# A sliding-window copy on one core: early tiles made of two columns, another mix of skipped rows, a second queue for the last stores

## The chip, the core and the metric

The kernel runs on one core of one Trainium2 chip. The metric is device time in microseconds, the median of several executions. The core has a vector engine (DVE), a scalar engine (ACT), GpSimd (POOL), a sync engine (SP) and a tensor engine that is not used here. Sixteen DMA engines move data between the memory outside (DRAM) and the 128 partitions of the memory on the chip. DMAs are issued by SP, ACT or POOL, each on its own queue; an indirect DMA, whose rows go to addresses read from an index tile, is issued by POOL.

## The reference

All windows of 8 x 8, at stride 4, are copied out of an input of 16 batches, 64 channels and 64 x 64 points. Nothing is calculated; each input value appears in up to four windows.

```python
batch, c, h, w = x.shape                       # 16, 64, 64, 64, float32
n_h = (h - window_size) // stride + 1          # 15
n_w = (w - window_size) // stride + 1          # 15
for i in range(n_h):
    for j in range(n_w):
        result[:, i, j] = x[:, :, 4*i:4*i + 8, 4*j:4*j + 8]
```

The input has 16.8 MB and the output 59.0 MB. One window of one batch, 64 channels x 64 values, is a row of 16 KB that lies in one piece in the output: 3600 such rows.

## The kernel before, in words

**Where the input lies.** The whole input is loaded once into the tile L (L49). A partition holds one channel half (ch, 32 channels), one batch and one quarter of the image height (q, 16 rows of points): partition = 64 ch + 32 y + 4 b + q, where y is the batch half and b one of its eight batches. The 16 rows of a quarter begin four windows, called slots s = 0 to 3; slot 3 needs rows of the next quarter also, and the last quarter has no slot 3.

**Loads.** L104 to L110 load y by y and q by q. Of channel half 0, SP issues channels SMALL to 31 and POOL the first SMALL channels (L54, SMALL = 4); POOL issues all of channel half 1. Each such load writes 8 partitions in pieces of 4 KB.

**Output tiles.** G is four tiles of 128 partitions x 4096 values, 16 KB in each partition: 128 output rows. tile_ (L160) hands them out in turn, so a tile's next use waits until its last store has landed. fill (L135) copies the two channel halves of one output row out of L, on ACT (act) and DVE (dve); copies of slot 3 take a copy and a stream_shuffle on DVE (L146, L147), which fetches from the next partition. scatter (L123) is one indirect DMA from POOL that sends the partitions of a tile to the rows named in an index tile; an index past the end makes it skip that row.

**Which tiles there are.** unit(j, 0) is a "plain" tile: column j, slots 0 and 1 of everything, 128 rows. unit(j, 2) is a "crossed" tile: slots 2 and 3; the last quarter has no slot 3, so 16 of its rows are skipped. In crossed tiles either partitions 64 to 127 hold slot 3 (idx_hi) or partitions 0 to 63 do (idx_lo); L182 chooses: 9 times idx_hi, 6 times idx_lo. part(y, j) is a tile of one batch half only, which can begin before the other half is loaded: 64 rows are filled and 64 skipped, by an index moved past the end (L89 to L93). The four tiles are filled with zeros first (L154 to L157), so that skipped partitions hold something.

**Order.** L188 to L199: part(0, j) for j = 0, 1, 2; then part(1, j) and a plain tile, three times; then two crossed tiles and a plain one, over and over: 32 scatters. Column 14 of slots 0 and 1 comes last: two tiles, each stored by four plain DMAs of 16 rows from SP (L214). tile_ is called once without use ahead of them. All stores write rows of their own and are declared free of each other.

The DMAs of POOL share eight completion semaphores in turn. A load or scatter waits until the one eight earlier has landed.

Of the kernel before, what the change touches and what calls it, by code (L numbers as in the profile page):

```python
# [10 lines left out]
def kernel(  # L11
# [7 lines left out]
    nc = tc.nc  # L19
    P = nc.NUM_PARTITIONS  # L20

    B, C, H, W = x.shape
    Bo, NH, NW, Co, WSo, WSo2 = out.shape
    WS = int(window_size)
    ST = int(stride)
    assert Bo == B and Co == C and WSo == WS and WSo2 == WS

    f32 = mybir.dt.float32
    i32 = mybir.dt.int32
    ALU = mybir.AluOpType  # L30
    CH = 2
    HQ = P // (B * CH)
    CL = C // CH
    RB = H // HQ
    NSLOT = RB // ST
    NWIN = NH * NW
    CFREE = C * WS * WS
    HP = P // CH
    YB = 8
    NY = B // YB  # L40
    QP = YB * HQ
# [3 lines left out]
    ipool = ctx.enter_context(tc.tile_pool(name="ipool", bufs=1))  # L45
# [3 lines left out]
    L = lpool.tile([P, CL, RB, W], f32)  # L49
# [1 line left out]

    SMALL, HWP = 4, 8  # L54

    def load(eng, ch, y, q, c0, c1):
        p0 = ch * HP + y * QP + q
# [4 lines left out]
    def itile(name):  # L62
        return ipool.tile([P, 1], i32, name=name)

    pi, tb, tq, tc_, th, idx, idx_y0, idx_y1, idx_lo, idx_hi = (
        itile(n) for n in ("pi", "tb", "tq", "tc", "th", "idx", "idx_y0", "idx_y1", "idx_lo", "idx_hi")
    )
    FAR = float(2 * B * NWIN)
    nc.gpsimd.iota(pi[:, :], pattern=[[0, 1]], base=0, channel_multiplier=1)  # L69

    def bits(d, shift, mask):
        nc.vector.tensor_scalar(out=d[:, :], in0=pi[:, :], scalar1=shift, scalar2=mask, op0=ALU.logical_shift_right, op1=ALU.bitwise_and)  # L72

    def mul(d, a, m):
        nc.vector.tensor_scalar(out=d[:, :], in0=a[:, :], scalar1=float(m), scalar2=None, op0=ALU.mult)  # L75

    def tt(d, a, b, op):
        nc.vector.tensor_tensor(out=d[:, :], in0=a[:, :], in1=b[:, :], op=op)  # L78
# [8 lines left out]
    tt(idx, tb, th, ALU.add)  # L87

    bits(th, 5, 1)  # L89
    mul(th, th, FAR)  # L90
    tt(idx_y0, idx, th, ALU.add)
    nc.vector.tensor_scalar(out=th[:, :], in0=th[:, :], scalar1=-1.0, scalar2=FAR, op0=ALU.mult, op1=ALU.add)
    tt(idx_y1, idx, th, ALU.add)  # L93

    nc.vector.tensor_scalar(out=tq[:, :], in0=tq[:, :], scalar1=float(HQ - 1), scalar2=FAR, op0=ALU.is_equal, op1=ALU.mult)
    tt(th, tc_, tq, ALU.mult)
# [17 lines left out]
    NG = 4  # L114
    G = [gpool.tile([P, C, WS, WS], f32, name=f"G{n}") for n in range(NG)]

    o_q = out.rearrange("b i j c r w -> i j b (c r w)")

    def free(st):
        tc.declare_no_dep(st.ins, group="stores", reason="each store writes rows of its own")  # L120
        tc.add_to_no_dep_group("stores", st.ins)

    def scatter(g, ix, j, s):  # L123
        st = nc.gpsimd.indirect_dma_start(  # L124
            out=o_v,
            out_offset=bass.IndirectOffsetOnAxis(ap=ix[:, 0:1], axis=0),
            in_=g.rearrange("p c r w -> p (c r w)"),
            in_offset=None,
            element_offset=(s * NW + j) * CFREE,
            bounds_check=B * NWIN - 1,  # L130
            oob_is_err=False,
        )
        free(st)

    def fill(g, half, s, j, lo, n, copies):  # L135

        d = slice(half * HP + lo, half * HP + lo + n)
        cols = slice(j * ST, j * ST + WS)
        for ch in (half, 1 - half):
            f = slice(ch * HP + lo, ch * HP + lo + n)  # L140
            cs = slice(ch * CL, (ch + 1) * CL)
            copy = copies[ch != half]
            if s < NSLOT - 1:
                copy(out=g[d, cs, :, :], in_=L[f, :, s * ST : s * ST + WS, cols])  # L144
            else:
                copy(out=g[d, cs, 0:ST, :], in_=L[f, :, s * ST : RB, cols])  # L146
                nc.vector.stream_shuffle(out=g[d, cs, ST:WS, :], in_=L[f, :, 0:ST, cols], mask=nxt)  # L147

    act, dve = nc.scalar.copy, nc.vector.tensor_copy

    EARLY = NG - 1
    zero = ipool.tile([P, 1], f32, name="zero")  # L154
    nc.vector.memset(zero[:, :], 0.0)  # L155
    for g in G:
        act(out=g.rearrange("p c r w -> p (c r w)"), in_=zero.to_broadcast([P, CFREE]))  # L157
    at = 0

    def tile_():  # L160
        nonlocal at
        at += 1
        return G[(at - 1) % NG]

    def part(y, j):
        g = tile_()
        for half in range(CH):
            fill(g, half, half, j, y * QP, QP, (dve, dve) if y and half else (act, dve))
        scatter(g, (idx_y0, idx_y1)[y], j, 0)

    crossed = 0

    def unit(j, s):
        nonlocal crossed
        g = tile_()
        if s == 0:
            for half in range(CH):
                fill(g, half, half, j, 0, HP, (act, dve))
            scatter(g, idx, j, s)
        else:  # L180

            turn = int(crossed % 5 in (1, 3))  # L182
            crossed += 1
            fill(g, turn, s, j, 0, HP, (act, act))
            fill(g, 1 - turn, s + 1, j, 0, HP, (dve, dve))
            scatter(g, (idx_hi, idx_lo)[turn], j, s)

    for j in range(EARLY):  # L188
        part(0, j)
    plain = [(j, 0) for j in range(EARLY, NW - 1)]  # L190
    cross = [(j, 2) for j in range(NW)]
    for j in range(EARLY):
        part(1, j)
        unit(*plain.pop(0))
    while plain:
        for w in cross[:2]:
            unit(*w)
        cross = cross[2:]
        unit(*plain.pop(0))  # L199


    j = NW - 1
    tile_()
    for s in range(2):
        g = tile_()
        cols = slice(j * ST, j * ST + WS)
        for y in range(NY):
            d = slice(QP + y * QP, QP + (y + 1) * QP)
            for ch, copy in enumerate((act, dve)):
                f = slice(ch * HP + y * QP, ch * HP + (y + 1) * QP)  # L210
                copy(out=g[d, ch * CL : (ch + 1) * CL, :, :], in_=L[f, :, s * ST : s * ST + WS, cols])  # L211
        g_q = g.rearrange("p c r w -> p (c r w)")
        for q in range(HQ):
            free(nc.sync.dma_start(out=o_q[q * NSLOT + s, j], in_=g_q[QP + q : QP + q + (B - 1) * HQ + 1 : HQ]))  # L214


# [33 lines left out]
```

## Time and profile before

| What | Value |
|---|---|
| median of 3 runs | 194.87 us (194.72 to 194.99) |
| the profiled execution | 194.68 us, of it 192.9 us span |
| DVE busy | 110.2 us (57%), 153 instructions |
| ACT busy | 138.3 us (72%), 70 instructions |
| POOL busy | 54.6 us (28%), 53 instructions |
| ACT copies of L144 | 61, 1896 ns each |
| DVE copies of L144 | 37, 1224 ns each |
| zero fills on ACT, L157 | 4, 3600 ns each |
| ACT_TABLE_LOAD, L157 | 1, 1283 ns, at 0.74 us |

The span is the time from the first to the last instruction of the profiled execution. An engine's busy time says how much it worked, not that it set the time: what matters is which of them the others waited for in each stretch. "idle before, releaser" tells what ended an engine's waits:

```profile
L144 ACT COPY G<-L 64x2048 f32<-64x2048 f32 (+1 forms) x61 | 115.3, 1896 | 40.0 <-issue 20.7
L147 DVE STREAM_SHUFFLE G<-L 64x1024 f32<-64x1024 f32 x30 | 38.3, 1277 | 0.0
L124 POOL DMA_INDIRECT out_dram<-G,idx_hi x9 | 12.0, 1338 | 34.9 <-DVE G L147 24.5
L157 ACT COPY G<-zero 128x4096 f32<-128x4096 f32 x4 | 14.1, 3600 | 0.0
```

Each line gives the source line, the engine, what is written and read, how often; then busy time, the mean of one in ns, and the idle time just before.

### The profile page before, as it was taken

Reading aid. Unit: us, or ns where it says so; the run is one execution under the profiler, and the core shown is the slowest. Engines: PE = TensorE matmul, PEld = TensorE weight load, DVE = VectorE, ACT = ScalarE, POOL = GpSimd, SP = SyncE. Lnnn points to the kernel's source line nnn. Section 1 sums busy time; section 2 is a strip of 40 time slices with the busy share of each in tenths; the row PEclk is TensorE's granted clock in tenths of the full one; section 3 lists DMA queues with packets and bytes.
Section 4 is the critical chain, followed back from the end, with each engine's and each line's share of the span. In section 5 each row is a group of like instructions: output and inputs, shape, how many; then the busy total and the mean of one; then the engine's idle time right before and its main releaser. Section 6 shows DMA issues by size and latency. Waiting matters only on the chain.

```text
span 192.9 us, 487 instructions
## 1 busy us (share of the span) xinstructions
DVE 110.2 (57%) x153; ACT 138.3 (72%) x70; POOL 54.6 (28%) x53
## 2 busy tenths in 40 slices
DVE  5000007700999979876876875874974794723330
ACT  8993008940897879999778777877977797754560
POOL 7402212531166430422214123134043124320000
DMA  2999999999989999999999999999999999999764
GB/s 79 337 404 400 399 401 397 401 401 407 421 357 418 404 423 421 425 421 404 426 425 428 420 411 418 432 435 411 404 435 418 425 431 404 418 432 435 321 292 177
DMA packets 11588, 75.81 MB, mean 393 GB/s; under 512 B 3888, under 2 KB 3888, under 8 KB 7984
## 3 DMA queue, kind: packets, MB, share of 16 engines
q0 software_dynamic: 9472, 66.34, 83.8%
q1 hardware_dynamic: 2112, 9.44, 12.4%
q14 instruction: 4, 0.03, 0.0%
HBM read 16.78 MB, written 69.21 MB: 446 GB/s over the span
## 4 chain that ended last, share of the span: by engine, by line
DMA 73%; DVE 12%; issue 7%; POOL 2%; ACTq 1%; ACT 1%; DVEq 0%; PEldq 0%
DMA out_dram<-G,idx 34%; DMA out_dram<-G,idx_hi 22%; DMA L<-in_x_dram 16%; DVE G L144 9%; POOL L L58 2%; DVE G L146 2%; DVE G L147 2%; ACTq L245 1%; ACT G L211 1%; DVEq L144 0%; POOL pi L69 0%; DVEq L146 0%; PEldq L245 0%; ACTq L211 0%
## 5 line engine op out<-in xcount | busy, mean ns | idle before, releaser
L144 ACT COPY G<-L 64x2048 f32<-64x2048 f32 (+1 forms) x61 | 115.3, 1896 | 40.0 <-issue 20.7
L144 DVE COPY G<-L 64x2048 f32<-64x2048 f32 (+1 forms) x37 | 45.0, 1224 | 41.9 <-DMA L<-in_x_dram 27.1
L147 DVE STREAM_SHUFFLE G<-L 64x1024 f32<-64x1024 f32 x30 | 38.3, 1277 | 0.0
L146 DVE COPY G<-L 64x1024 f32<-64x1024 f32 x30 | 21.6, 720 | 21.5 <-DMA out_dram<-G,idx 16.2
L124 POOL DMA_INDIRECT out_dram<-G,idx_hi x9 | 12.0, 1338 | 34.9 <-DVE G L147 24.5
L58 POOL DMA_DIRECT2D L<-in_x_dram x16 | 11.4, 715 | 23.9 <-DMA L<-in_x_dram 23.4
L124 POOL DMA_INDIRECT out_dram<-G,idx x11 | 12.4, 1126 | 18.6 <-ACT G L144 15.9
L124 POOL DMA_INDIRECT out_dram<-G,idx_lo x6 | 8.9, 1480 | 24.1 <-DVE G L147 17.0
L124 POOL DMA_INDIRECT out_dram<-G,idx_y x6 | 9.6, 1603 | 16.0 <-ACT G L144 8.9
L157 ACT COPY G<-zero 128x4096 f32<-128x4096 f32 x4 | 14.1, 3600 | 0.0
L211 ACT COPY G<-L 32x2048 f32<-32x2048 f32 x4 | 7.6, 1896 | 7.4 <-DMA out_dram<-G,idx 4.9
L211 DVE COPY G<-L 32x2048 f32<-32x2048 f32 x4 | 4.9, 1220 | 10.1 <-DMA out_dram<-G,idx 6.6
L157 ACT ACT_TABLE_LOAD x1 | 1.3, 1283 | 0.7 <-PEq L231 0.7
L155 DVE MEMSET zero<- 128x1 f32 x1 | 0.1, 59 | 0.8 <-PEq L231 0.8
L78 DVE CUSTOM_DVE_ANT_0 idx_y<-idx,th 128x2 uint16<-128x2 uint16 x2 | 0.3, 160 | 0.1
L78 DVE TENSOR_TENSOR th<-tc,tq 128x1 int32<-128x1 int32 x2 | 0.3, 158 | 0.1
L75 DVE TENSOR_SCALAR th<-tc 128x1 int32<-128x1 int32 x2 | 0.3, 154 | 0.0
L69 POOL IOTA pi<- 128x1 int32 x1 | 0.1, 125 | 0.4 <-PEq L245 0.4
L72 DVE TENSOR_SCALAR tb<-pi 128x1 int32<-128x1 int32 x1 | 0.2, 154 | 0.1
L147 DVE LOAD_MASK_SELECT G<-L x30 | 0.2, 6 | 0.0
L78 DVE CUSTOM_DVE_ANT_0 idx_hi<-idx,th 128x2 uint16<-128x2 uint16 x1 | 0.2, 160 | 0.0
L78 DVE CUSTOM_DVE_ANT_0 idx<-tb,th 128x2 uint16<-128x2 uint16 x1 | 0.2, 159 | 0.0
(16 smaller groups left out, 2.2 us busy)
## 6 DMA issues: line engine op xcount, KB each, us to landing
L<-in_x_dram POOLq DMA_DIRECT2D x8, 1024.0 KB, 21.0
L<-in_x_dram SPq DMA_DIRECT2D x8, 896.0 KB
out_dram<-G SPq DMA_DIRECT2D x8, 256.0 KB
L<-in_x_dram POOLq DMA_DIRECT2D x8, 128.0 KB, 21.1
out_dram<-G,idx POOLq DMA_INDIRECT x11, 14.5
out_dram<-G,idx_hi POOLq DMA_INDIRECT x9, 14.1
out_dram<-G,idx_y POOLq DMA_INDIRECT x6, 9.8
out_dram<-G,idx_lo POOLq DMA_INDIRECT x6, 12.9
```

Source lines behind the costliest of these rows:

```text
L58: eng.dma_start(out=L[p0 : p0 + QP - HQ + 1 : HQ, c0:c1, :, :], in_=x_v[ch, y, q, :, c0:c1, :])
L69: nc.gpsimd.iota(pi[:, :], pattern=[[0, 1]], base=0, channel_multiplier=1)
L72: nc.vector.tensor_scalar(out=d[:, :], in0=pi[:, :], scalar1=shift, scalar2=mask, op0=ALU.logical_shift_right, op1=ALU.bitwise_and)
L75: nc.vector.tensor_scalar(out=d[:, :], in0=a[:, :], scalar1=float(m), scalar2=None, op0=ALU.mult)
L78: nc.vector.tensor_tensor(out=d[:, :], in0=a[:, :], in1=b[:, :], op=op)
L124: st = nc.gpsimd.indirect_dma_start(out=o_v, out_offset=bass.IndirectOffsetOnAxis(ap=ix[:, 0:1], axis=0), in_=g.rearrange("p c r w -> p (c ...
L144: copy(out=g[d, cs, :, :], in_=L[f, :, s * ST : s * ST + WS, cols])
L146: copy(out=g[d, cs, 0:ST, :], in_=L[f, :, s * ST : RB, cols])
L147: nc.vector.stream_shuffle(out=g[d, cs, ST:WS, :], in_=L[f, :, 0:ST, cols], mask=nxt)
L157: act(out=g.rearrange("p c r w -> p (c r w)"), in_=zero.to_broadcast([P, CFREE]))
L211: copy(out=g[d, ch * CL : (ch + 1) * CL, :, :], in_=L[f, :, s * ST : s * ST + WS, cols])
L245: with _tile.TileContext(nc) as tc:
```

## The change

- SMALL is 1: SP loads 31 channels of channel half 0 and POOL one.
- part(y, j) fills all 128 partitions: for its batch half, slots 0 and 1 of columns j and j + 1, in eight copies of 32 partitions, four on ACT and four on DVE. The index tiles idx_y0 and idx_y1 name rows of both columns (column + 1 in place of batch + 8), and none is skipped. It is called for j = 0, 2, 4, so the six early tiles cover columns 0 to 5, and plain tiles begin at column 6. There are 29 scatters.
- The zero fills are gone.
- Crossed tiles take idx_hi and idx_lo in turn (8 and 7), and three of them stand between two plain ones.
- Of the last four DMAs two are issued by ACT, two by SP.

```diff
-    SMALL, HWP = 4, 8
+    SMALL, HWP = 1, 8
...
     bits(th, 5, 1)
-    mul(th, th, FAR)
-    tt(idx_y0, idx, th, ALU.add)
-    nc.vector.tensor_scalar(out=th[:, :], in0=th[:, :], scalar1=-1.0, scalar2=FAR, op0=ALU.mult, op1=ALU.add)
-    tt(idx_y1, idx, th, ALU.add)
+    mul(idx_y0, th, 1 - YB * NWIN)
+    tt(idx_y0, idx_y0, idx, ALU.add)
+    nc.vector.tensor_scalar(out=idx_y1[:, :], in0=idx_y0[:, :], scalar1=float(YB * NWIN), scalar2=None, op0=ALU.add)
...
-    EARLY = NG - 1
-    zero = ipool.tile([P, 1], f32, name="zero")
-    nc.vector.memset(zero[:, :], 0.0)
-    for g in G:
-        act(out=g.rearrange("p c r w -> p (c r w)"), in_=zero.to_broadcast([P, CFREE]))
+    EARLY = 3
...
     def part(y, j):
         g = tile_()
-        for half in range(CH):
-            fill(g, half, half, j, y * QP, QP, (dve, dve) if y and half else (act, dve))
+        for d in range(P // QP):
+            s, dj = d // NY, d % NY
+            cols = slice((j + dj) * ST, (j + dj) * ST + WS)
+            for ch in range(CH):
+                f = (ch * NY + y) * QP
+                (act, dve)[(d + ch) % 2](
+                    out=g[d * QP : (d + 1) * QP, ch * CL : (ch + 1) * CL, :, :],
+                    in_=L[f : f + QP, :, s * ST : s * ST + WS, cols],
+                )
         scatter(g, (idx_y0, idx_y1)[y], j, 0)
...
-            turn = int(crossed % 5 in (1, 3))
+            turn = crossed % 2
...
-    for j in range(EARLY):
-        part(0, j)
-    plain = [(j, 0) for j in range(EARLY, NW - 1)]
+    for n in range(EARLY):
+        part(0, 2 * n)
+    plain = [(j, 0) for j in range(2 * EARLY, NW - 1)]
     cross = [(j, 2) for j in range(NW)]
-    for j in range(EARLY):
-        part(1, j)
+    for n in range(EARLY):
+        part(1, 2 * n)
         unit(*plain.pop(0))
     while plain:
-        for w in cross[:2]:
+        for w in cross[:3]:
             unit(*w)
-        cross = cross[2:]
+        cross = cross[3:]
         unit(*plain.pop(0))
...
-            free(nc.sync.dma_start(out=o_q[q * NSLOT + s, j], in_=g_q[QP + q : QP + q + (B - 1) * HQ + 1 : HQ]))
+            free((nc.sync, nc.scalar)[s * q % 2].dma_start(out=o_q[q * NSLOT + s, j], in_=g_q[QP + q : QP + q + (B - 1) * HQ + 1 : HQ]))
```

## The prediction, made blind

> **What bounds the kernel now.** I read the page first (its slices, DMA packets and queues), then the stretches of time, then the timeline of POOL and ACT, and last the completion records of the trace, in which each of the 16 DMA engines reports the end of its share of a transfer.
>
> ```profile
> DMA  2999999999989999999999999999999999999764
> DMA packets 11588, 75.81 MB, mean 393 GB/s; under 512 B 3888, under 2 KB 3888, under 8 KB 7984
> q0 software_dynamic: 9472, 66.34, 83.8%
> q1 hardware_dynamic: 2112, 9.44, 12.4%
> ```
>
> The DMA engines are busy from the second slice to the 37th. They are the bound; ACT and DVE only have to feed them. The change moves the same 75.81 MB, so it can win only where the engines idle (the start, one dip, the last three slices) or where one carries more than another.
>
> ```profile
> 25.00:46.00 21.00, 7.11 (x6) 10.99 (x6) 7.43 (x6) 1.00 1.04 397
> 46.00:54.00 8.00, 5.90 (x5) 5.61 (x3) 1.52 (x1) 1.00 1.04 426
> 54.00:60.00 6.00, 5.84 (x6) 5.90 (x5) 3.46 (x3) 1.00 0.85 352
> 60.00:176.00 116.00, 83.69 (x112) 92.82 (x49) 33.91 (x27) 1.00 1.01 422
> 176.00:187.00 11.00, 4.88 (x4) 7.58 (x4) 0.00 (x0) 1.00 0.79 331
> 187.00:193.00 6.00, 0.00 (x0) 0.00 (x0) 0.00 (x0) 1.00 0.48 202
> ```
>
> The last two columns are DMA share and GB/s. Loads run at 397 GB/s, or 24.8 an engine: 0.165 us for a 4 KB packet. Scatters run at 422, or 26.4 an engine: 0.62 us for a 16 KB row. The dip is at 54 to 60 us (0.85: 0.9 us lost). At the end the share falls to 0.79 and 0.48: half of the engines are done. In the completion records, eight engines end the last scatter at 180.4 us, seven at 186.6 to 186.9, one at 188.5; the last transfer ends on seven at 191.0 and on that one at 192.0.
>
> ```profile
> 14.49 0.66 POOL L58 DMA_DIRECT2D L<-in_x_dram  x1 [4.81 <-DMA L<-in_x_dram]
> 21.20 0.66 POOL L58 DMA_DIRECT2D L<-in_x_dram  x1 [4.87 <-DMA L<-in_x_dram]
> 28.05 0.66 POOL L58 DMA_DIRECT2D L<-in_x_dram  x1 [4.86 <-DMA L<-in_x_dram]
> 34.91 1.31 POOL L58 DMA_DIRECT2D L<-in_x_dram  x1 [3.99 <-DMA L<-in_x_dram]
> 29.52 11.01 ACT L144 COPY G<-L 32x2048 f32<-32x2048 f32 x6 [13.36 <-issue]
> 50.27 11.51 ACT L144 COPY G<-L 64x2048 f32<-64x2048 f32 x6 [0.46 <-DMA out_dram<-G,idx_y]
> ```
>
> POOL reissues a load when the one eight earlier has landed, so its lines show the landings of the first batch half: a round every 6.8 us, the last at 34.6. ACT starts its copies at 29.52, when channel half 0 is there. One ACT copy costs 11.01/6 = 1.84 us early and 11.51/6 = 1.92 us later.
>
> [...] POOL's large loads end on one half 5.2 us apart (32 packets at 0.163). [...] q0's 9472 packets less 3472 rows, 2304 load packets, 768 reports and 624 skipped rows leave 2304 empty packets, one in group A for each load packet in B and the reverse. A round on A is 4 small packets and 4 of SP's, then 32 empty ones turn about with 32 of SP's: 40 x 0.165 = 6.6 us, seen 6.8. [...]
>
> **SMALL 4 to 1.** A round on A becomes 1 + 1, then 32 + 32 with 34 data packets: 6 x 0.165 = 1.0 us less. Channel half 1 of the first batch half (34.6) is whole 4 rounds, 4.0 us, earlier: 30.6. For half 0 the small loads end at 29.2 - 4.0 = 25.2. SP's fourth load ended at 25.1 after 112 of its packets and 12 of POOL's; now it is 124 and 4, four slots more: 25.1 + 0.7 + 0.2 for empty packets = 26.0. Each engine still carries 256 load packets, so the second half stays at about 47.8 and scatter data begins at 46.7 as before.
>
> **Zero fills out, table load moved.** The four fills (14.1 us of ACT from 2.04) lay beside an ACT idle until 29.5: worth nothing. But the ACT_TABLE_LOAD had them behind it; now it stands before the first copy and carries seven of that copy's waits for loads. Its 1.28 us fall after 26.0. The index arithmetic loses one DVE instruction of 0.15 us and the memset of 0.06, before 4 us: nothing, since DVE waits until 26.
>
> **Full tiles.** Before, a first-half tile took ACT 2 copies, a second-half one 1, a plain one 2. Now a paired tile takes 4 copies of ACT and 4 of DVE (4 x 1.24 = 5.0 us, less than ACT's), and there are 29 scatters, not 32, for the same 3472 rows; skipped rows are packets of 9 ns in the packet records, so the 384 that go save 0.2 us an engine at most, and I take 0. ACT: first copy at 27.3; six for half 0 to 38.3; then two a tile: tiles 0, 1, 2 done at 42.0, 45.6, 49.3. By then the second half is there. Tile 3 takes 7.7 us: 57.0; plain 4 60.8; paired 5 68.5; plain 6 72.3; paired 7 80.0; plain 8 83.9; crossed 9 87.7. From POOL's issue to data I take 2.6 us: the scatter issued at 52.48 (POOL 1.86) landed its 4 rows an engine by 57.9, so data began at 55.1; where POOL takes 0.96, 1.7. DMA wants a tile every 8 x 0.62 = 4.96 us from 46.7: tile 3 at 61.6, 4 at 66.5, 5 at 71.5, 6 at 76.5, 7 at 81.4, 8 at 86.4 (plus any stall), 9 at 91.3. Ready: 59.6, 63.4, 71.1, 74.9, 82.6, 86.5, 90.3. Only tile 7 is late, by 1.2 us, or 0.3 at the short latency; I take 0.8. Before, the dip cost group A 1.0 us (54.2 to 55.1 and 57.5). Net -0.2. After tile 9 ACT makes a tile in 3.84 us and the queue fills again; buffers (tile k-4 landed) are free each time, tile 7's at 66.8 against 72.3.
>
> **Skipped rows shared.** Rows of one A engine before: 11 plain x 8 + 6 halves x 4 + 15 crossed x 8 - 6 x 2 + 8 final = 228; of B the same with 9 x 2 skipped, 222. After: 8 x 8 + 6 x 8 + 120 - 7 x 2 + 8 = 226, and 224. Group A ends the run: 46.6 + 1.0 + 228 x 0.628 = 190.8, which fits its 191.0 (0.628 is the pace fitted from its completions). Two rows less: -1.26 us. B would end at 47.2 + 0.8 + 224 x 0.62 = 186.9, still earlier.
>
> **Two queues.** The final eight ran on A one behind another, 186.5, 187.1, ... 191.0, spaced 0.6 to 0.7: an engine's row time, not SP's issue. Two of the last four issued by ACT behind its last copies gain nothing on A. No row shows an ACT issue: at worst SP's 1.38 for one, at best -0.2 as the last rows close up; I take 0.
>
> **Sum.** -1.26 - 0.2 + 0 = -1.5 on the span of 192.9: 191.4. The profiled execution took 194.68, 1.78 around its span; that gives 193.2, and the median of the runs (194.87) stands 0.19 over it: 193.3.
>
> **The rivals.** (1) Slower by ACT: the early stretch has 1 us to spare and no more. Every microsecond that channel half 0, the table load or a copy is late goes into the wait before tile 7. If half 0 comes at 29.5 as before, tile 7 is 4.7 late, not 1.0: +3.7 - 1.26, 197.3. It decides from about 1.1 us of lateness (idle 2.25 in all). For it: ACT leaves no gap from 27 to 88. Against: the counted packets. (2) Slower by the loads: should a one-channel load not turn the cursor, half of the large loads fall on A: 128 packets x 0.165 = +21 us there, about 214. [...] (3) A wash: tile 7's full 1.2 us, and a straggler like that at 192.0 grown by 1: 194.87 + 0.2 - 1.26 + 1.0 = 194.8. (4) Better: that straggler (+1.0 us at the end, first seen at 182.5 in the scatter before the last, beside a 0.3 us instruction fetch at 181.1) falls elsewhere: 192.3.
>
> **How the numbers follow.** Forecast 0.49, with its own range 192.3 to 194.4 (early net from -1.0 to +0.9). Rival 1 0.21, 2 0.08, 3 0.13, 4 0.09. Low 192.0 holds rival 4; high 197.5 takes in most of rival 1 and leaves out rival 2. About 0.2% (0.4 us) is what a measurement tells from no change: faster is the forecast less its upper edge and rival 4, 0.56; same 0.13; slower 0.31.
>
> **What would show it.** Right: ACT's table load at 26, copies without a gap until about 88; POOL's load rounds 5.8 us apart; first scatter issued at 42; DMA share 1.0 but for a notch near 82; the eight early engines done about 3 us later than 180.4 and the other eight 1.5 us earlier; the final transfers ending near 189.5 on seven engines and 190.5 on the last. Wrong: copies first at 29 or later, a second dip before tile 5, large loads on both groups, or the last engine at 192 as before.

## The result, and the profile after

The changed kernel takes 217.33 us (median of 4 runs, 217.07 to 217.74) beside 194.92 us for the kernel before in the same runs: ratio 1.1154, with a 95% interval of 1.1131 to 1.1177. The forecast of 193.3 was wrong, in sign and in size. The profiled execution has a span of 215.8 us against 192.9, so 22.9 us are to be found.

The slices of the page of the changed kernel, 5.4 us each, show where. For the kernel before the prediction shows the first and the third of these lines.

```profile
DMA  3999579559799957969999999999999999999984
GB/s 97 276 268 282 208 254 272 202 208 285 234 400 424 390 216 334 437 289 430 431 416 431 422 421 430 425 413 416 437 410 416 425 425 428 398 437 422 418 346 176
DMA packets 10964, 75.81 MB, mean 351 GB/s; under 512 B 3264, under 2 KB 3264, under 8 KB 7360
```

The line of GB/s of the kernel before (slices of 4.8 us) and one of its stretches of time are:

```profile
GB/s 79 337 404 400 399 401 397 401 401 407 421 357 418 404 423 421 425 421 404 426 425 428 420 411 418 432 435 411 404 435 418 425 431 404 418 432 435 321 292 177
5.00:25.00 20.00, 0.00 (x0) 11.16 (x4) 4.45 (x8) 1.00 1.03 388
```

The bytes are the same, 75.81 MB. Before, the third to the eleventh slice moved 397 to 421 GB/s. Now the second to the eleventh move 202 to 285, with stretches in which the engines are only half busy. From slice 19 (97 us) on the two kernels look alike. So the loss begins in the load stage. The stretches of time of the changed kernel (DVE, ACT and POOL busy, clock, then DMA share and GB/s) say the same:

```profile
5.00:20.00 15.00, 0.00 (x0) 0.00 (x0) 2.01 (x4) 1.00 0.98 272
20.00:30.00 10.00, 0.00 (x0) 0.00 (x0) 2.42 (x4) 1.00 0.64 224
75.00:100.00 25.00, 19.49 (x17) 24.69 (x14) 6.97 (x4) 1.00 0.78 330
100.00:200.00 100.00, 71.66 (x103) 85.24 (x46) 26.25 (x22) 1.00 1.01 422
```

Two things are wrong in the load stage. From 20 to 30 us the share is 0.64: one half of the engines has no work for most of it. By the packet records only eight packets are under way at a time from 22 to 30 us, from 38 to 49 and around 58. And from 5 to 20 us all engines are busy (0.98), but move only 272 GB/s, against 388 before: the packets themselves are slower. The share of 0.78 from 75 to 100 us is what follows from it: the half of the engines that was done with its loads early has stored the first three tiles by 75.4 us and stands still until 83.9, when the fourth is ready; the other half stores without a break. From 100 us on a row costs about what it did (422 GB/s in both kernels).

The timeline of POOL and ACT in the changed kernel shows what followed. POOL reissues a load about 0.3 us after the one eight earlier has landed:

```profile
7.13 0.53 POOL L58 DMA_DIRECT2D L<-in_x_dram  x1 [0.64 <-DMA L<-in_x_dram]
22.82 1.21 POOL L58 DMA_DIRECT2D L<-in_x_dram  x2 [15.16 <-DMA L<-in_x_dram]
28.31 1.21 POOL L58 DMA_DIRECT2D L<-in_x_dram  x2 [4.28 <-DMA L<-in_x_dram]
41.18 1.81 POOL L58 DMA_DIRECT2D L<-in_x_dram  x2 [11.65 <-DMA L<-in_x_dram]
41.55 1.28 ACT L166 ACT_TABLE_LOAD   x1 [41.55 <-DMA L<-in_x_dram]
42.85 22.96 ACT L166 COPY G<-L 32x2048 f32<-32x2048 f32 x12
46.62 1.47 POOL L58 DMA_DIRECT2D L<-in_x_dram  x1 [3.63 <-DMA L<-in_x_dram]
73.98 1.90 ACT L166 COPY G<-L 32x2048 f32<-32x2048 f32 x1 [8.18 <-issue]
```

Before, the large loads landed in even rounds of 6.8 us. Now the first four land at 22.5, 28.0, 40.9 and 46.3 us, a short step of 5.5 us and a long one of 12.9 in turn. (The line at 7.13 follows the landing of a one-channel load.) Channel half 0 of the first batch half comes at 41.5 (29.5 before, 26.0 forecast). ACT's copies of the second half begin at 73.98 (47.91 before). The 1.28 us of the table load are there, where the forecast had put them.

The completion records tell which engines did what; they carry no engine numbers, so the groups are read from the times. A load of SP has eight of them, a load of POOL sixteen. The first large load reports from eight engines at 4.1 us, too early for data (POOL's first packet of 4 KB starts at 5.8), and from the other eight, which have its data, at 21 to 22.5. The second has its data on the first eight, 14.9 to 15.3, and the other eight report at 27 to 28. The third is as the first, the fourth as the second. So the large loads now fall on the two groups of engines in turn. Group A is the half with the first large load, B the other. A also carries SP's loads: from 25 to 30 us, with B idle, 176 load packets of SP start and 82 of POOL. The first two one-channel loads report from B at 3.0 and 4.4 us, too early for data there also, so all eight are counted on A, as an estimate: A gets 248 + 8 + 4 x 32 = 384 packets an engine, and B 4 x 32 = 128. Before it was 256 each.

Group A's last load ends near 73.1 us. Its scatter data begins at 73.3, against 46.6 before: +26.7. From there the working of the prediction holds: 226 rows instead of 228 (-1.26), no dip on A, since it has a queue of ready tiles (-1.0), and a pace of (213.6 - 73.3)/226 = 0.621 us a row instead of the 0.628 of before (-1.6). The sum is +22.8, and 22.9 were measured. The pace is fitted to the end, so the sum nearly closes by construction; what it shows is that the late start of A, +26.7, is the loss, and that all that comes after it is a gain of 3.9.

### The profile page after: what moved, and what is told of

It is laid out like the page before. It is cut to its first block, busy times and chain, and to the rows that moved or that the text cites. A ratio compares the mean times of both kernels' runs of the same rounds, so it can differ in the third digit from the quotient of the medians.

```text
span 215.8 us, 482 instructions
## 1 busy us (share of the span) xinstructions
DVE 113.0 (52%) x154; ACT 141.5 (66%) x75; POOL 47.9 (22%) x50
## 2 busy tenths in 40 slices
DMA packets 10964, 75.81 MB, mean 351 GB/s; under 512 B 3264, under 2 KB 3264, under 8 KB 7360
## 4 chain that ended last, share of the span: by engine, by line
DMA 75%; issue 11%; DVE 4%; ACT 3%; POOL 3%; POOLq 0%; DVEq 0%; ACTq 0%; PEldq 0%
DMA L<-in_x_dram 28%; DMA out_dram<-G,idx_hi 25%; DMA out_dram<-G,idx 10%; DMA out_dram<-G,idx_lo 6%; DMA out_dram<-G,idx_y 5%; DVE G L166 2%; POOL L L58 2%; ACT G L212 2%; ACT G L143 1%; DVE G L143 1%; POOL out_dram L123 1%; DVE G L146 1%; DVE G L145 0%; POOLq L123 0%; POOL pi L69 0%
## 5 line engine op out<-in xcount | busy, mean ns | idle before, releaser
L143 ACT COPY G<-L 64x2048 f32<-64x2048 f32 x46 | 87.2, 1897 | 9.8 <-DMA out_dram<-G,idx 4.5
L166 DVE COPY G<-L 32x2048 f32<-32x2048 f32 x24 | 29.3, 1223 | 60.3 <-DMA L<-in_x_dram 55.4
L166 ACT COPY G<-L 32x2048 f32<-32x2048 f32 x24 | 45.5, 1896 | 8.7 <-issue 8.2
L145 DVE COPY G<-L 64x1024 f32<-64x1024 f32 x30 | 20.8, 692 | 16.4 <-DMA out_dram<-G,idx_hi 9.3
L143 DVE COPY G<-L 64x2048 f32<-64x2048 f32 x16 | 19.6, 1222 | 6.6 <-DMA out_dram<-G,idx 6.3
L123 POOL DMA_INDIRECT out_dram<-G,idx_y x6 | 7.4, 1236 | 42.6 <-ACT G L166 42.6
L123 POOL DMA_INDIRECT out_dram<-G,idx_hi x8 | 10.5, 1312 | 22.9 <-ACT G L143 17.4
L123 POOL DMA_INDIRECT out_dram<-G,idx x8 | 10.0, 1248 | 20.7 <-ACT G L143 19.3
L123 POOL DMA_INDIRECT out_dram<-G,idx_lo x7 | 8.4, 1193 | 24.7 <-DVE G L146 18.9
L212 ACT COPY G<-L 32x2048 f32<-32x2048 f32 x4 | 7.6, 1896 | 7.3 <-DMA out_dram<-G,idx_lo 5.0
L212 DVE COPY G<-L 32x2048 f32<-32x2048 f32 x4 | 4.9, 1220 | 10.0 <-DMA out_dram<-G,idx_lo 6.3
```

The costliest lines, as they stand in the source:

```text
L123: st = nc.gpsimd.indirect_dma_start(out=o_v, out_offset=bass.IndirectOffsetOnAxis(ap=ix[:, 0:1], axis=0), in_=g.rearrange("p c r w -> p (c ...
L166: (act, dve)[(d + ch) % 2](out=g[d * QP : (d + 1) * QP, ch * CL : (ch + 1) * CL, :, :], in_=L[f : f + QP, :, s * ST : s * ST + WS, cols],)
```

## The experiments

Twelve kernels were run. Three theories stood at the start. **Cursor**: POOL's loads take eight engines at a time in turn, as if a cursor pointed to the next eight; a one-channel load does not turn it, so the large loads alternate. **Share**: SP's 31 channels of 32, or the one-channel loads themselves, delay the loads. **Early tiles**: the paired tiles cost the time through ACT.

### SMALL alone, both ways

The changed kernel with SMALL at 4:

```diff
-    SMALL, HWP = 1, 8
+    SMALL, HWP = 4, 8
```

> The changed kernel with SMALL back at 4. Cursor theory (a one-channel load on POOL does not turn the choice of engines, so the large loads fall on both groups in turn): POOL's large loads are all on one group again, the last load lands near 48 us and the loss of 22 us is gone. The first batch half then comes at 29.5 and 34.6 us as before the change, the table load adds 1.3, so by the working of the prediction tiles 5 and 7 come 3.2 and 1.6 us late: about 197. Early-tile theory (the paired tiles themselves cost the time, by ACT): stays over 210. Share theory (SP's 31 channels are what delays the loads): near 195, since SP has 28 again; it differs from the cursor theory in the run without small loads.

Measured: 197.27 us, ratio to before 1.0127 (1.011 to 1.0143). Of the loss of 22.4 us, 20.1 are gone. What is left is the price of the early tiles where the loads come as late as before, which the prediction had worked out as its first rival (197.3). Its timeline of POOL has the even rounds again, and ACT starts at 29.58 with the table load:

```profile
14.65 0.66 POOL L58 DMA_DIRECT2D L<-in_x_dram  x1 [5.00 <-DMA L<-in_x_dram]
21.34 0.66 POOL L58 DMA_DIRECT2D L<-in_x_dram  x1 [4.88 <-DMA L<-in_x_dram]
28.21 0.66 POOL L58 DMA_DIRECT2D L<-in_x_dram  x1 [4.88 <-DMA L<-in_x_dram]
...
29.58 1.28 ACT L166 ACT_TABLE_LOAD   x1 [29.58 <-DMA L<-in_x_dram]
```

The kernel before with SMALL at 1 and nothing else:

```diff
-    SMALL, HWP = 4, 8
+    SMALL, HWP = 1, 8
```

> The kernel before with SMALL at 1 and nothing else. Cursor theory: 128 packets of 0.165 us more on one group of engines, 21 us: about 214 to 217. Early-tile theory: about 195 or a little less, since the first half comes earlier. Share theory: 210 or more too.

Measured: 220.87 us, 1.1337 (1.1318 to 1.1356). One digit costs the old kernel 26 us, with its half-filled tiles and zero fills untouched, and POOL's reissues follow the landings at 22.7, 28.2, 41.1 and 46.5 us, as in the changed kernel. The early-tile theory falls with these two runs.

The changed kernel with SMALL at 2:

```diff
-    SMALL, HWP = 1, 8
+    SMALL, HWP = 2, 8
```

> The changed kernel with SMALL at 2. Cursor theory, if two channels are enough to turn the cursor: large loads on one group, a round of the first half 36 slots of 0.165 us, so half 0 is there at 26.6 and half 1 at 32.0; tile 7 about 1.8 us late; about 194.4. If two channels do not turn it: about 217 as with one. Share theory: about 210, since SP carries 30 of 32 channels. Early-tile theory: over 210.

Measured: 194.84 us, 1.0000 (0.9992 to 1.0009). With 30 of 32 channels on SP the loss is not there. The share theory, which had 210 here, falls. Two pieces of 4 KB a partition turn the cursor, one does not: in the completion records the large loads have their data on one group of eight engines again, at 11.2, 16.3, 21.4 and 26.6 us. ACT starts at 26.75; the forecast of rounds of 36 slots had said 26.6.

### What the one-channel load does to the cursor

The changed kernel with SP loading all 32 channels of half 0, so that POOL issues large loads only:

```diff
-    SMALL, HWP = 1, 8
+    SMALL, HWP = 0, 8
...
-            load(nc.gpsimd, 0, y, q, 0, SMALL if hw else CL)
```

> The changed kernel with SP loading all 32 channels of half 0, so that POOL issues the eight large loads only. Cursor theory: the large loads follow each other directly and take the two groups in turn, as they do now: 216 to 219, no different from the changed kernel. Share theory: no different from 217 either, or a little slower. A theory in which the one-channel loads themselves cost the time (their packets or reports): near 195.

Measured: 215.41 us, 1.1059 (1.1034 to 1.1084), 2 us less than with the one-channel loads. The completion records alternate as in the changed kernel. So to the large loads that follow, a one-channel load is as good as absent.

The one-channel loads kept, with a load of 1 KB added ahead of each large one:

```diff
+    turn_t = [ipool.tile([P, 2, 16], f32, name=f"turn{k}") for k in range(NY * HQ)]
...
+            k = y * HQ + q
+            nc.gpsimd.dma_start(out=turn_t[k][0:QP // HQ, :, :], in_=x_v[0, y, q, :, 0:2, 0:16])
```

> The changed kernel, its one-channel loads kept, with one more POOL load of 1 KB ahead of each large one: 8 partitions, two pieces of 64 bytes each, to a tile that nothing reads. Cursor theory: the small extra load turns the choice of engines, the large loads stay on one group, and the 22 us are gone: about 195 (a round on the shared engines has 36 slots, as with SMALL at 2). Any theory in which the shares of SP and POOL, or the one-channel loads themselves, cost the time: 217 or a little more.

Measured: 194.49 us, 0.9987 (0.9978 to 0.9997). Eight loads of 1 KB, which nothing reads, bring back 22.8 us. They change no share and move no byte of the large loads. They do change when POOL issues, since 24 loads now share the eight semaphores, but the completion records show that the place is what changed: the large loads have their data on one group of eight engines at 11.5, 16.6, 21.8 and 27.0 us, 5.2 us apart as in the kernel before. Its timeline has an even step of 6 us between turns, and ACT starts at 26.71:

```profile
14.12 0.58 POOL L111 DMA_DIRECT2D turn<-in_x_dram  x1 [5.82 <-DMA L<-in_x_dram]
20.38 0.58 POOL L111 DMA_DIRECT2D turn<-in_x_dram  x1 [4.47 <-DMA L<-in_x_dram]
26.44 1.62 POOL L111 DMA_DIRECT2D turn<-in_x_dram  x1 [4.27 <-DMA L<-in_x_dram]
...
26.71 1.28 ACT L169 ACT_TABLE_LOAD   x1 [26.71 <-DMA L<-in_x_dram]
```

That a one-channel load leaves the choice of engines where it was, and that this is the loss, is shown: 217.33 us with one channel and 194.84 with two, 215.41 with large loads alone and 194.49 with the loads of 1 KB. Why it does so is not.

### The other parts, one at a time

The skipped rows alone, on the kernel before:

```diff
-            turn = int(crossed % 5 in (1, 3))
+            turn = crossed % 2
```

> The kernel before with idx_hi and idx_lo in turn and nothing else. Prediction: group A carries two rows less, 2 x 0.63 = 1.26 us: 193.6. Rival (the end is set by the straggling engine or by the chain of the last tile): within 0.4 us of 194.8.

Measured: 193.68 us, 0.9943 (0.9929 to 0.9956): 1.1 us for two rows of one group. Between 176 and 187 us its engines are busy 0.86 of the time, against 0.79 before, since the two groups now end nearer together: in the completion records the last scatter ends near 181.8 us on one and from 185.6 on the other, where it was 180.4 and 186.6:

```profile
176.00:187.00 11.00, 4.61 (x4) 6.93 (x4) 0.00 (x0) 1.00 0.86 364
```

One end moves 1.4 us later and the other 1.0 earlier with one tile changed from idx_hi to idx_lo, so the two skip rows of different groups, as the prediction had estimated.

The two queues alone, on the kernel before:

```diff
-            free(nc.sync.dma_start(...))
+            free((nc.sync, nc.scalar)[s * q % 2].dma_start(...))
```

> The kernel before with two of the last four transfers issued by ACT and nothing else. Prediction: nothing, since the engines of group A take them one behind another at their row time: 194.6 to 194.9. Rival (SP's issue spacing sets the end): 193.6 to 194.2.

Measured: 195.21 us, 1.0021 (1.001 to 1.0031): a loss of 0.4 us rather than nothing. The last landings are at 191.3 and 192.3 in place of 191.0 and 192.0: issue was not what held the end, and a second queue makes the same rows end a little later. Why it does was not tried.

The table load ahead of the loads, with SMALL at 2:

```diff
+    one = ipool.tile([P, 1], f32, name="one")
+    two = ipool.tile([P, 1], f32, name="two")
+    nc.vector.memset(one[:, :], 0.0)
+    act(out=two[:, :], in_=one[:, :])
```

> The changed kernel with SMALL at 2 and a copy of one element on ACT at the start, so that the table load is done before the loads land. Theory of the prediction (ACT's path to tiles 5 and 7 is the only loss of the early stretch): the first copy comes 1.3 us earlier, the DMA engines' wait of about 1.9 us before tiles 5 and 7 shrinks to about 0.7, so 193.6 against 194.8 with the table load late. Rival (these waits are made up for later, since the end is set elsewhere): 194.8, no change.

Measured: 191.9 us, 0.9847 (0.9833 to 0.986): 2.9 us better than SMALL at 2, where 1.2 were expected. The surplus had another cause. In this run the middle value of the 16 KB row packets, from the packet records between 100 and 20 us before the end, was 611 ns; in all earlier ones it was 618. The two new tiles had moved the four G tiles in memory, from 192 to 0 bytes past a multiple of 256. This was then tried by itself, in the kernel before:

```diff
     zero = ipool.tile([P, 1], f32, name="zero")
+    pad = ipool.tile([P, 1], f32, name="pad")
+    nc.vector.memset(pad[:, :], 0.0)
```

> The kernel before with one unused tile of 4 bytes a partition more, which moves the four G tiles from 224 to 0 bytes past a multiple of 256; nothing else. In the run with SMALL at 2 and the early table load the G tiles had moved to such a place too, and its 16 KB row packets took 611 ns in the middle value against 618 in all other runs. Theory (the start address makes the rows cheaper): rows at 611, 228 rows x about 8 ns = 1.8 us less, about 193.0. Rival (the packets were faster for another reason): 194.8.

Measured: 193.0 us, 0.9908 (0.9893 to 0.9923), rows at 611 ns. From 60 to 176 us it moves 427 GB/s, where the kernel before moved 422:

```profile
60.00:176.00 116.00, 83.56 (x113) 93.11 (x50) 33.62 (x27) 1.00 1.01 427
```

Two unused tiles in the changed kernel with SMALL at 2, and the table load left late:

```diff
-    SMALL, HWP = 1, 8
+    SMALL, HWP = 2, 8
...
+    for n in range(2):
+        pad = ipool.tile([P, 1], f32, name=f"pad{n}")
+        nc.vector.memset(pad[:, :], 0.0)
```

> The changed kernel with SMALL at 2 and two unused tiles, so that G starts at a multiple of 256 bytes, the table load left late. If the address is worth 1.8 us: 193.0, and the early table load is worth the 1.1 us that remain to 191.9. If the address is worth nothing: 194.8, and the table load was worth all 2.9 us.

Measured: 193.25 us, 0.9918 (0.9903 to 0.9934). So the address is worth 194.84 - 193.25 = 1.6 us here, and the early table load 193.25 - 191.9 = 1.35 us, about its own 1.28.

### A version that beats both

The paired tiles with three copies on ACT and five on DVE, SMALL at 2, table load early, G at a multiple of 256 bytes:

```diff
-                (act, dve)[(d + ch) % 2](
+                (dve if d == 3 else (act, dve)[(d + ch) % 2])(
```

> SMALL at 2, the early table load, and in paired tiles three copies on ACT and five on DVE in place of four and four (5.8 and 6.2 us in place of 7.7 and 5.0). If ACT's path is what makes tiles 5 and 7 late: the remaining wait of about 0.8 us goes, about 191.1. If not: 191.9.

Measured: 189.16 us, 0.9713 (0.9698 to 0.9728), 2.7 us less than with four and four, where 0.8 were expected. The stretch from 70 to 90 us shows the wait that went; the first line is the run with four and four, the second with three and five:

```profile
70.00:90.00 20.00, 14.84 (x20) 19.76 (x11) 7.38 (x5) 1.00 0.91 390
```

```profile
70.00:90.00 20.00, 16.60 (x24) 17.50 (x10) 5.90 (x5) 1.00 1.01 433
```

ACT was busy 19.76 of 20 us in the first and has gaps in the second; the DMA share goes from 0.91 to 1.01, which is 2.0 us at most; by the packet records the engines idled 1.7 us in the first. The rest is in the pace: the mean row, over the same stretch before the end as above, falls from 616.6 to 611.5 ns, 226 x 5.1 = 1.2 us.

The same with all final transfers on SP:

```diff
-            free((nc.sync, nc.scalar)[s * q % 2].dma_start(...))
+            free(nc.sync.dma_start(...))
```

> The same with all eight final transfers issued by SP. If the second queue costs what it cost the kernel before (0.4 us): 190.7. If it costs nothing here: no different from the run with five copies on DVE.

Measured: 188.78 us, 0.969 (0.9678 to 0.9703), the best of all: 6.0 us better than the kernel before. The second queue cost 0.4 us here too.

## Why the prediction was wrong

**The step that failed** stands under "SMALL 4 to 1": "Each engine still carries 256 load packets, so the second half stays at about 47.8 and scatter data begins at 46.7 as before." It is 384 on group A and 128 on group B, the second half came at 74.0, and scatter data began on A at 73.3. The prediction took the four-channel loads for what turns the cursor, and that a one-channel load does so too was the author's estimate. The possibility stood as rival 2, with a chance of 0.08 and "about 214". Its mechanism is what happened, and its price was near, in part by luck: it reckoned +21 us for 128 packets at 0.165, and group A took 26.7 us more, because packets were slower too (over all loads, a mean of 221 ns for POOL's and 179 for SP's, against 168 and 169 before); against that, the gains after the load stage came to 3.9 us where the forecast had 1.5. An edit that no row of the trace shows in its new form, and on which 21 us hang, deserved more than 0.08 and a place in the range.

**The rounds.** A round was to be shorter by the small packets that it no longer has. Right as long as the cursor turns: with SMALL at 2, ACT starts at 26.75, for 26.6 worked out. That empty packets of POOL's queue and packets of SP's take turns, on which the working rests, is in the packet records of the kernel before: between 10 and 20 us, 407 of SP's 449 packets of 4 KB begin 4 to 7 ns after the beginning of a 4-byte packet of POOL's queue.

**Full tiles and the table load.** Right in the main. With the loads as late as before, 197.3 was worked out and 197.27 measured; that it fits so well is luck, since the 197.27 has the second queue's 0.4 us in it, which the working took as nothing. The table load on ACT's path costs 1.35 us for the 1.28 of its row. The forecast's "1 us to spare and no more" is what SMALL at 2 and 4 show: 194.84 and 197.27.

**Zero fills.** Costed at nothing behind ACT's idle time, and not tried alone; the sums of the runs above close without them.

**Skipped rows shared.** -1.26 worked out, -1.1 measured alone.

**Two queues.** 0 taken, from -0.2 to a loss of 1.4 for one issue; measured +0.4.

**The sum without the failing step.** The forecast's own terms add up to 193.4 (191.4 + 1.78 + 0.19), not 193.3. With SMALL at 2 the same working gives 194.4, and 194.84 was measured; the 0.4 us between them are as much as the second queue cost alone. So apart from the cursor the terms of the sum hold, to about 0.4 us. With one channel and a turning cursor the changed kernel itself could not be run: the added loads that turn it lengthen the rounds to those of SMALL at 2.

## What to carry to other kernels

A size that looks like a tuning number may also decide which engines carry a transfer, as the 26 us for SMALL at 1 in the kernel before show: before making a transfer smaller, ask what it does besides moving bytes, and look in the completion records at which engines carry the next one. Here the end was set by the DMA engines with the most to carry (384 load packets an engine on A, 128 on B), so count rows and packets by engine, and set each producer's time for a tile against the DMA time of that tile. A store tile's start address and an instruction that inherits another's waits (here the table load) are cheap to set right: 1.8 and 1.35 us of 195.

## What the runs showed that was not expected

**Address of the source.** Rows of 16 KB leave in 611 ns (middle value) from tiles that start at a multiple of 256 bytes, and in 618 from tiles 192 or 224 bytes past one. The mean is 615.8 against 624.0 in the kernel before with and without the unused tile. No run tried another place, so whether 256 is the step that counts, and not 128 or 512, is open. Why rows from such places take 1.1% longer in the middle value, and 1.3% in the mean, was not shown.

**Slow load packets.** While the large loads alternate, a 4 KB packet of POOL takes 248 ns between 10 and 20 us and SP's takes 223, where both take 164 in the kernel before (means). The engines are fully busy then, at 272 GB/s. From 25 to 30 us, where half of the engines idle, SP's take 159. In the slow stretch two large loads run at once on the two groups and write partitions out of the same 32, where in the kernel before one large load followed another on one group; whether that is the cause was not tried.

**Engines out of step.** In the runs with three and five copies no stall stops all engines at once, their ends stay spread over 1 us from 50 us on, and the mean row is 611.5 ns. In the run with four and four the engines all restart together after the waits near 72 and 82 us, and the mean is 616.6 at the same addresses. Whether the common restart is what makes the rows dearer was not tried by itself.
